# A hybrid attention, Mamba and expert layer on one core: the compressed branch moved into the compression stage, u loaded back in the attention stage, one more weight slot, and another order of the last expert pieces

## Chip, core and metric

The kernel runs on 1 core of one Trainium2 chip. The metric is device time in microseconds (us): the median of several executions. Engines are named as the profile names them: PE (TensorE), DVE (VectorE), ACT (ScalarE), POOL (GpSimd), SP (SyncE, which here issues most DMAs).

## What is computed

One layer over a prompt of 256 tokens and 8 samples of 8 tokens (320 rows of 1024). Cut to what matters here:

```python
xn = rmsnorm(x); q, kv, ag, z, xbc, dt, mg = split(xn @ w_in)
kc, vc = compress(cmp rows)                      # a row per 16 tokens, from blocks of 32
o_c = softmax(q @ kc.T - slope * dist) @ vc      # compressed branch
A = gate_c * o_c + gate_s * o_sel + gate_w * o_win
u = silu(causal_conv(xbc)); M = gated_norm(ssd_scan(u, dt), z)
h = x + (sigmoid(g_a) * (A @ Wa) + sigmoid(g_m) * (M @ Wm)) @ W_out
y = h + sum over the 2 experts (of 32) of each row: (silu(hn @ Wg) * (hn @ Wu)) @ Wd * weight
```

All is float32; where it says hi and lo below, a float32 matrix is split into two parts for three fast products in place of a slow one.

## The kernel before

The stages follow each other: x and the first projections (0 to 95 us); the compression of the caches of 8 samples and of the prompt (`st_cmp`, to 228); attention of the prompt (`st_prompt`, to 310); attention of the samples (`st_att`, to 421); the SSD (`st_ssd`); the merge and the output projection; the router; the experts (`ph_moe`, from 648 to the end).

Beside the middle stages runs a second stream, the fill (`st_fill`): the rest of the combined projection as 24 matmuls per tile of 128 columns, `mm<-xh,whl` and `mm<-xl,whl`. A tile needs its weights loaded (`w`, 1 MB for two tiles, two buffers, issued on SP) and split: hi by ACT (L342), lo by DVE (L343), into `whl`. `_drive` (L135) draws from the streams by costs written at each `yield`, and the framework's scheduler then fixes one order of instructions per engine. Each engine runs its own order strictly in a row, so an instruction that waits holds up all behind it on that engine. The same goes for a DMA that waits on the queue of SP.

The compressed branch of the prompt stands at the start of `st_prompt` (L929 ff.): PE multiplies KC and qT into tile `at`; DVE adds the distances (tile `PP` of `Pc`, L944), reduces (L945), clips, subtracts (L947) and scales (L951); ACT takes exp; DVE sums, inverts, applies the gate and normalises (L953 to L959, statistics in tile `cst`); PE transposes the result and ACT copies it to `PcT`, which every block of the prompt's attention then reads (`pv<-PcT,vcp`). The distances come by a DMA of 512 KB in `ph_b_setup` (L638). `q2_parts` (L650) splits q: ACT copies hi, POOL subtracts. Then follow 16 blocks of scores (`at<-K,q`), a fused add and maximum on DVE (L782 with tile `pmx`), exps on ACT, normalising, transposes (`tp<-PP`) and products (`pv`).

`ph_b2_setup` (L785) loads for the samples' attention the constants `cB` (932 KB) and `P`, after which `wraw` (512 KB) and the eight parts of `raw` follow, all on SP.

The fill writes u, the convolution's result, to DRAM (`ud`) and, per four feature tiles, the last raw rows (`cv`, L1110 ff.) to the outputs. `ph_c_setup` (L1146) loads half of u back (2 DMAs of 640 KB on ACT's queue) as the SSD starts; the SSD transposes it (`tp<-cA,u`).

The experts' weights come through a ring of 1 MB pieces: per expert four pieces of gate and up, (e,0) to (e,3), and two of down, (e,4) and (e,5). `RING_SLOTS` (L32) counts 18 slots. Pieces are loaded in the order of `rseq` (L1415 ff.), a piece when its slot is free; the first 18 while the stages ahead still run. Experts go in pairs; `gu` multiplies a piece when it is there, `turn` transposes, `down` multiplies the down pieces, `parts` splits the result, `scatters` adds it to the rows. In the last pair, `last_down` works with halves of columns. `back` (L1767) computes the scatter matrix and coefficients of a pair with small float32 products of `cr`.

## Time and profile before

| what | us |
|---|---|
| median of 3 runs | 1119.47 (1118.45 to 1124.41) |
| the profiled execution | 1119.53 |
| its span | 1117.8 |
| PE busy in it | 1057.1 |
| DVE busy in it | 618.2 |
| ACT busy in it | 409.6 |
| experts, from 648 us on | 470 |

The profiled execution lasted 1.7 us more than the span that the profile covers, and lies 0.06 us from the median. PE is busy in 95% of the span. An idle gap in a timeline stands in brackets behind the work that follows it, with what was waited for.

### The profile page before, as it was taken

How to read it: one execution, taken by the hardware profiler on the slowest of the kernel's cores; microseconds unless marked ns; L12 is line 12 of the kernel's file. 1: busy time of each engine (PE TensorE's matmuls, PEld its weight loads, DVE VectorE, ACT ScalarE, POOL GpSimd, SP SyncE). 2: the span in 40 equal slices, each digit the busy share in tenths (PEclk: the TensorE clock that was granted, in tenths of full speed). 3: DMA queues.
4: the chain of work that ended last, by engine and by line, in shares of the span. 5: the costliest groups of instructions: out<-in, count | busy, mean ns of one | idle time of the engine just before them, and what ended most of it. 6: DMA issues, size and time to landing. Idle time of an engine off the chain costs nothing.

```text
span 1117.8 us, 18377 instructions
## 1 busy us (share of the span) xinstructions
PE 1057.1 (95%) x6743; PEld 728.9 (65%) x6743; DVE 618.2 (55%) x1686; ACT 409.6 (37%) x959; POOL 85.0 (8%) x115
## 2 busy tenths in 40 slices
PE   6998999969999998999999989999999999999997
PEld 6898899957776787777899944354444444435333
DVE  4467777788867774578876532333434333333324
ACT  4446565677745452545545511110101010101101
POOL 3102000042200001024100000000000000000000
PEclk8999999989999998999999999999999999999999
DMA  7844555511266656584579969999999999999995
GB/s 213 229 139 141 164 153 155 149 56 55 87 181 204 196 153 191 155 229 91 138 267 342 375 211 411 413 414 413 411 412 414 413 414 413 412 412 414 413 413 197
DMA packets 141742, 298.01 MB, mean 267 GB/s; under 512 B 14918, under 2 KB 93222, under 8 KB 133970
## 3 DMA queue, kind: packets, MB, share of 16 engines
q1 hardware_dynamic: 135146, 283.34, 70.7%
q0 software_dynamic: 2688, 7.91, 2.3%
q10 hardware_dynamic: 3816, 5.56, 1.6%
q8 instruction: 55, 0.90, 0.3%
q14 instruction: 37, 0.30, 0.1%
HBM read 279.63 MB, written 15.29 MB: 264 GB/s over the span
## 4 chain that ended last, share of the span: by engine, by line


## 5 line engine op out<-in xcount | busy, mean ns | idle before, releaser
L215 PE MATMUL mm<-xh,whl 128*128 128x320 f32 (+1 forms) x1008 | 248.8, 326 | 7.6 <-ACT whl L342 4.4
L215 PEld LDWEIGHTS mm<-xh,whl 128*128 128x128 f32 (+1 forms) x1008 | 173.5, 191 | 21.1 <-issue 7.9
L215 PE MATMUL mm<-wr,xeT 128*64 128x512 f32 x752 | 171.8, 595 | 4.8 <-DMA wr<-in_w_exp_up 3.0
L215 PE MATMUL mm<-xl,whl 128*128 128x320 f32 (+1 forms) x504 | 162.9, 323 | 0.0
L215 PEld LDWEIGHTS mm<-wr,xeT 128*64 128x64 f32 x752 | 53.5, 137 | 109.8 <-issue 103.6
L215 PE MATMUL po<-wr,ehT 128*64 128x512 f32 (+1 forms) x448 | 118.5, 580 | 4.2 <-DMA wr<-in_w_exp_down 4.2
L343 DVE TENSOR_TENSOR whl<-w,whl 128x1024 fp32r<-128x1024 f32 (+1 forms) x79 | 96.0, 1217 | 23.7 <-ACT whl L342 22.5
L1805 DVE SCALAR_TENSOR_TENSOR eth<-eth,mm 128x256 f32<-128x256 f32 x31 | 13.1, 421 | 170.6 <-ACT eth L1804 170.6
L342 ACT ACTIVATE whl<-w 128x1024 fp32r<-128x1024 f32 (+1 forms) x79 | 83.1, 1055 | 45.8 <-PE mm L215 38.5
L215 PEld LDWEIGHTS mm<-xl,whl 128*128 128x128 f32 (+1 forms) x504 | 96.3, 191 | 3.3 <-issue 1.6
L1804 ACT ACTIVATE eth<-mm,cb 128x256 f32<-128x256 f32 x31 | 14.7, 475 | 201.0 <-PE mm L215 201.0
L215 PEld LDWEIGHTS po<-wr,ehT 128*64 128x64 f32 x448 | 37.3, 137 | 72.3 <-issue 60.3
L1858 DVE TENSOR_TENSOR ht<-sc,ht 128x512 f32<-128x512 f32 (+3 forms) x99 | 61.7, 665 | 38.7 <-PE sc L215 38.2
L215 PE MATMUL mm<-ah,whl 128*128 128x320 f32 x256 | 63.9, 322 | 0.0
L346 DVE SCALAR_TENSOR_TENSOR olo<-po,cb,ohi 128x512 fp32r<-128x512 f32 (+1 forms) x33 | 24.2, 734 | 49.7 <-ACT ohi L345 49.7
L1780 ACT ACTIVATE ohT<-tp 128x320 fp32r<-128x320 f32 x16 | 7.0, 437 | 106.1 <-PE sc L215 98.3
L215 PEld LDWEIGHTS mm<-ah,whl 128*128 128x128 f32 x256 | 43.9, 188 | 2.0 <-issue 0.7
L215 PE MATMUL tp<-oh,hh 128*128 128x256 f32 x192 | 42.2, 292 | 0.0
L215 PE MATMUL sc<-ohi,ohT 128*128 128x512 f32 (+3 forms) x99 | 41.5, 421 | 0.2
L345 ACT ACTIVATE ohi<-po,cb 128x512 fp32r<-128x512 f32 (+1 forms) x33 | 22.2, 674 | 53.1 <-PE po L215 53.1
L215 PE MATMUL mm<-al,whl 128*128 128x320 f32 x128 | 39.6, 309 | 0.0
L215 PEld LDWEIGHTS tp<-oh,hh 128*128 128x128 f32 x192 | 32.9, 188 | 9.0 <-issue 8.1
(491 smaller groups left out, 1895.0 us busy)
## 6 DMA issues: line engine op xcount, KB each, us to landing
wr<-in_w_exp_down SPq DMA_DIRECT2D x50, 1024.0 KB
wr<-in_w_exp_gate SPq DMA_DIRECT2D x98, 512.0 KB
wr<-in_w_exp_up SPq DMA_DIRECT2D x98, 512.0 KB
w<-in_w_in SPq DMA_DIRECT2D x23, 1024.0 KB
raw<-in_cache_kv SPq DMA_DIRECT2D x112, 128.0 KB
w<-in_w_exp_down SPq DMA_DIRECT2D x10, 1024.0 KB
whl<-in_w_exp_gate SPq DMA_DIRECT2D x20, 512.0 KB
whl<-in_w_exp_up SPq DMA_DIRECT2D x20, 512.0 KB
```

Source lines behind the costliest of these rows:

```text
L215: return s.nc.tensor.matmul(out, lhsT, rhs, start=start, stop=stop, skip_group_check=True)
L342: s.last_split = [nc.scalar.activation(hi, src, AF.Copy), nc.vector.tensor_tensor(lo, src, hi.bitcast(F32), op=OP.subtract)]
L343: nc.vector.tensor_tensor(lo, src, hi.bitcast(F32), op=OP.subtract)]
L345: nc.scalar.activation(hi, src, AF.Copy, scale=scale)
L346: nc.vector.scalar_tensor_tensor(lo, src, scale, hi.bitcast(F32), op0=OP.mult, op1=OP.subtract)
L1780: nc.scalar.activation(t, p[:, 0:T], AF.Copy)
L1804: nc.scalar.activation(hv, g, AF.Tanh, scale=hrs)
L1805: nc.vector.scalar_tensor_tensor(hv, hv, 1.0, g, op0=OP.add, op1=OP.mult)
L1858: nc.vector.tensor_tensor(y, ps[:m], y, op=OP.add)
```

## The change

- `st_pc` is a stream of its own that runs beside `st_cmp` as soon as the prompt's compressed keys are there (flag "kc"); it holds the whole compressed branch up to `PcT`. Its tiles Pc, PcT and cst lie in a new tile `ux`, and the DMA of the distances is issued ahead of the compression. `st_prompt` starts with the splits of K and of the first two parts of q; later parts of q are issued after an exp.
- u is loaded into the same memory (`ux`) by `load_x`, issued on SP: from the fill's z tiles as soon as the flag "prompt" is set, so within the samples' attention.
- To make room in memory some tiles share a buffer or have fewer (`gt`, `PT`, `qt`, `si`); `cv` is written per two feature tiles, in eight pairs of small DMAs in place of four.
- `RING_SLOTS` counts 19. The pieces (28,5) and (29,5) are loaded ahead of the four gate and up pieces of expert 31, and the products with them (`rest`) stand ahead of its `gu`; half of the scatters of that pair stand inside it.
- In `back` the three products with `cr` take hi and lo parts (`crs`, split once in the router's second part), with six columns in place of three, and the copies behind them become sums of three columns.

```diff
-RING_SLOTS = (8, 5, 2, 2, 1)
+RING_SLOTS = (8, 5, 2, 2, 2)
...
-        s.Pc = s.tl(P, [128, 1024], F32, "PP", bufs=3)
-        o, n = s.bo["pC"]
-        nc.sync.dma_start(s.Pc, s.I["cB"][:, o:o + n])
...
+    def ph_pc_setup(s):
+        t = s.tl(s.pU, [128, 8 * T], F32, "ux")
+        s.Pc = t[:, 0:1024]
+        s.PcT = t[:, 1024:2048].rearrange("p (a b) -> p a b", b=128)
+        s.cst = t[:, 2048:2144].rearrange("p (a b) -> p a b", b=32)
+        nc.sync.dma_start(s.Pc, s.I["cB"][:, o:o + n])
+
+    def st_pc(s):
+        yield lambda: "kc" in s.flags
...
+        for qt in range(2):
+            p = s.ps("tp", [128, 512])
...
+                s.mm(p[:, r * 64:r * 64 + n], s.qT[:, r, qt * 128:(qt + 1) * 128], KC[:, 0:n], True, True)
+            nc.vector.tensor_tensor(Pc[:, qt * 512:(qt + 1) * 512], p, Pc[:, qt * 512:(qt + 1) * 512], op=OP.add)
+            yield 3000
+        nc.vector.tensor_reduce(stt[:, 0], Pv, axis=AX.X, op=OP.max)
...
+        nc.scalar.activation(Pc, Pc, AF.Exp)
...
+        for hh in range(2):
+            p = s.ps("tp", [128, 4, 128])
+            for u in range(4):
+                s.tr(p[:, u], Pc[:, (hh * 4 + u) * 128:(hh * 4 + u + 1) * 128])
+            nc.scalar.copy(s.PcT[:, hh * 4:hh * 4 + 4], p)
+            yield 3000
...
-                if r % 2 == 0 and qt == 1 and r < 6:
-                    s.q2_parts(r + 2, r + 4)
                 cur = probs(r, qt)
+                if r % 2 == 0 and qt == 1 and r < 6:
+                    s.q2_parts(r + 2, r + 4, s.last_exp)
...
                 nc.sync.dma_start(s.zd[m // 2][m % 2], z)
+                if "prompt" in s.flags:
+                    s.load_x()
...
+    def load_x(s):
+        if not hasattr(s, "u"):
+            s.u = s.tl(s.pU, [128, 8 * T], F32, "ux").rearrange("p (f t) -> p f t", t=T)
+            for k in range(2):
+                s.nc.sync.dma_start(s.u[:, 4 * k:4 * k + 4], s.ud[k].rearrange("f p t -> p f t"))
...
-        s.u = s.tl(P, [128, 8, T], F32, "u")
-        for k in range(2):
-            nc.scalar.dma_start(s.u[:, 4 * k:4 * k + 4], s.ud[k].rearrange("f p t -> p f t"))
...
+        s.rseq[-6:] = s.rseq[-2:] + s.rseq[-6:-2]
...
-                mm(p[:, 384:387], o[i], s.cr[:, i, e // 2], i == 0, i == 2)
+                mm(p[:, 384:390], o[i], s.crs[:, i, e // 2].rearrange("p a b -> p (a b)"), i == 0, i == 2)
...
+            if e == 30:
+                left = rest()
+                after[1] = lambda: scatters(left[0], left[1])
             hB = gu(e + 1, lambda: cb[:, 2:3], after, "mm" if prev else "po")
-            if prev:
-                down(pe, st["hT"], 1, po)
-                left = (pt, *(parts(pe, po[dh], pcb[:, 0:1], dh * 512, 512) for dh in range(2)))
+            if prev and e < 30:
+                left = rest()
...
-    _drive([s.st_cmp()], [fill], RATES[0])
+    _drive([s.st_cmp(), s.st_pc()], [fill], RATES[0])
```

What this does to the order on three engines:

DVE at the start of the prompt's attention, before. `cst` and the rows of `PP_2336` are the compressed branch; `PP_2502`, `pmx_2503` and `PP_2522` are the first blocks of scores, on which PE's next matmuls wait for room.

```order
338 L945 TENSOR_REDUCE cst_2351<-PP_2336 128x32
339 L782 ISA PP_2502,pmx_2503<-at_2504,Dp_2334 128x128
340 L782 ISA pmx_2503 128x1
341 L946 TENSOR_SCALAR cst_2351<-cst_2351 128x32
342 L782 ISA PP_2502,pmx_2503<-at_2504,Dp_2334 128x128
343 L782 ISA pmx_2503 128x1
344 L947 TENSOR_TENSOR PP_2336<-PP_2336,cst_2351 128x1024
345 L782 ISA PP_2502,pmx_2503<-at_2504,Dp_2334 128x128
346 L782 ISA pmx_2503 128x1
347 L951 TENSOR_TENSOR PP_2336<-PP_2336,cA_11_110 128x512 x2
348 L994 TENSOR_TENSOR pmx_2503<-pmx_2503,cA_11_110 128x4
349 L782 ISA PP_2522,pmx_2523<-at_2524,Dp_2334 128x256
```

DVE after the change, in the compression: `ux_984` holds Pc and cst, `whl`, `cvt` and `ut` belong to the fill, `gt`, `gx`, `kx` to the compression.

```order
189 L671 TENSOR_TENSOR ux_984<-tp_1475,ux_984 128x512
190 L1114 SCALAR_TENSOR_TENSOR ut_2609<-raw_2607,cvt_2451 128x256
191 L673 TENSOR_REDUCE ux_984<-ux_984 128x32
192 L1115 SCALAR_TENSOR_TENSOR ut_2609<-raw_2607,cvt_2451 128x64
193 L674 TENSOR_SCALAR ux_984<-ux_984 128x32
194 L1090 MEMSET raw_2680 128x3
195 L676 TENSOR_TENSOR ux_984<-ux_984 128x1024
196 L714 SCALAR_TENSOR_TENSOR gt_1560<-gt_1560,gx_1558 128x256
197 L681 TENSOR_TENSOR ux_984<-ux_984,cA_11_110 128x512
198 L716 SCALAR_TENSOR_TENSOR gx_1558<-gt_1560,gx_1558 128x256
199 L681 TENSOR_TENSOR ux_984<-ux_984,cA_11_110 128x512
200 L790 COPY kx_203<-tp_1565 128x2x64
```

DVE after the change, at the start of the prompt's attention (`PP_2474`, `PP_2517`: the second and the third block of scores; the split of `whl` that PE's fill needs next follows as row 370).

```order
348 L1013 TENSOR_TENSOR pmx_2407<-pmx_2407,cA_11_110 128x4
349 L834 ISA PP_2474,pmx_2475<-at_2476,Dp_2387 128x256
350 L834 ISA pmx_2475 128x1
351 L834 ISA PP_2474,pmx_2475<-at_2479,Dp_2387 128x256
352 L834 ISA pmx_2475 128x1
353 L834 ISA PP_2474,pmx_2475<-at_2479,Dp_2387 128x256
354 L834 ISA pmx_2475 128x1
355 L834 ISA PP_2517,pmx_2518<-at_2519,Dp_2387 128x128
356 L834 ISA pmx_2518 128x1
357 L1013 TENSOR_TENSOR pmx_2475<-pmx_2475,cA_11_110 128x4
```

The compressed branch has left the rows between the first blocks of scores and stands among the compression's and the fill's rows.

SP before, at the border to the samples' attention.

```order
225 L1125 DMA zd_6_96<-ut_4208 128x320
226 L790 DMA cB_3705<-in_cB 128x1864
227 L794 DMA P_3708<-in_cB 32x1024
228 L799 DMA wraw_3711<-in_cache_win_kv 128x1024
229 L799 DMA wraw_3713<-in_cache_win_kv 128x1024
```

SP there after the change; `ux_4030` is u, in the memory from which PE reads PcT until the prompt's last block.

```order
232 L1134 DMA out_conv_prompt<-cv_3669 3x256
233 L1135 DMA out_conv_sample<-cv_3669 24x256
234 L1172 DMA ux_4030<-ud_1_91 128x4x320
235 L842 DMA cB_3678<-in_cB 128x1864
236 L846 DMA P_3681<-in_cB 32x1024
237 L851 DMA wraw_3684<-in_cache_win_kv 128x1024
238 L851 DMA wraw_3686<-in_cache_win_kv 128x1024
```

The first load of u stands ahead of `cB`, `P` and `wraw` (the second follows as row 258, behind the first `wraw` and `raw`).

PE before, at the end: the four pieces of expert 31 (`mm_10477`), then the second down pieces of pair 28 (`po_10467`, wr_1735 and wr_1736).

```order
3154 L215 MATMUL mm_10477<-wr_1717_10257,xeT_10176 64x512 x4
3155 L215 MATMUL mm_10477<-wr_1718_10264,xeT_10190 64x512 x4
3156 L215 MATMUL mm_10477<-wr_1730_10318,xeT_10204 64x512 x4
3157 L215 MATMUL mm_10477<-wr_1731_10325,xeT_10218 64x512 x4
3158 L215 MATMUL po_10467<-wr_1735_10342,ehT_10441 64x512
3159 L215 MATMUL po_10467<-wr_1736_10344,ehT_10441 64x512
```

PE there after the change: the down pieces come first (`po_10489`), and six scatters (`sc`) stand between the second and the third piece of expert 31 (`mm_10514`).

```order
3160 L215 MATMUL po_10489<-wr_1719_10265,ehT_10462 64x512
3161 L215 MATMUL po_10489<-wr_1725_10280,ehT_10462 64x512
3162 L215 MATMUL mm_10514<-w_10286,xeT_10199 64x512 x4
3163 L215 MATMUL mm_10514<-w_10340,xeT_10213 64x512 x4
3164 L215 MATMUL sc_10523<-ohi_10506,ohT_10308 128x512
3165 L215 MATMUL sc_10523<-olo_10507,ohT_10308 128x512
3166 L215 MATMUL sc_10527<-ohi_10506,ohT_10308 128x512
3167 L215 MATMUL sc_10527<-olo_10507,ohT_10308 128x512
3168 L215 MATMUL sc_10531<-ohi_10506,ohT_10308 64x512
3169 L215 MATMUL sc_10531<-olo_10507,ohT_10308 64x512
3170 L215 MATMUL mm_10514<-whl_10347,xeT_10227 64x512 x4
3171 L215 MATMUL mm_10514<-whl_10364,xeT_10241 64x512 x4
```

Behind the last piece of expert 31 there are left six scatters, the transposes and the last down.

## Rows read from the trace of the kernel before

**Rows 1.** the page, part 1: engine, busy us (share of the span), instructions.

```profile
PE 1057.1 (95%) x6743; PEld 728.9 (65%) x6743; DVE 618.2 (55%) x1686; ACT 409.6 (37%) x959; POOL 85.0 (8%) x115
```

**Rows 2.** windows by stage: stretch, us, busy of each engine, granted clock, DMA share, GB/s.

```profile
95.00:228.00 133.00, 127.67 (x955) 120.83 (x955) 99.50 (x238) 81.02 (x208) 7.90 (x25) 0.97 0.50 151
228.00:310.00 82.00, 70.66 (x555) 53.86 (x556) 71.75 (x282) 59.72 (x191) 26.55 (x24) 0.92 0.16 51
```

**Rows 3.** timeline of PE after 231 us: start, duration, work, [idle before <-releaser].

```profile
235.12 0.51 PE L215 MATMUL at<-K,q 128*128 128x256 f32 x2 [0.73 <-POOL q L656]
...
238.34 0.42 PE L215 MATMUL mm<-xh,whl 128*128 128x320 f32 x1 [1.50 <-ACT whl L342]
...
240.55 0.76 PE L215 MATMUL at<-K,q 128*128 128x512 f32 x2 [1.65 <-DVE pmx L782]
245.52 2.05 PE L215 MATMUL at<-K,q 128*128 128x256 f32 x6 [4.21 <-DVE pmx L782]
250.60 0.90 PE L215 MATMUL mm<-xh,whl 128*128 128x320 f32 x2 [3.03 <-DVE whl L343]
```

**Rows 4.** windows of 5 us around both waits.

```profile
235.00:240.00 5.00, 2.29 (x11) 1.67 (x11) 4.33 (x9) 4.90 (x10) 4.70 (x5) 1.00 0.00 0
240.00:245.00 5.00, 0.76 (x2) 0.30 (x2) 5.00 (x9) 1.57 (x3) 4.52 (x3) 0.61 0.00 0
245.00:250.00 5.00, 2.05 (x6) 1.35 (x6) 5.00 (x21) 3.59 (x17) 0.41 (x1) 0.50 0.00 0
250.00:255.00 5.00, 4.18 (x19) 3.64 (x20) 5.00 (x13) 1.44 (x4) 2.17 (x2) 0.53 0.67 207
...
435.00:440.00 5.00, 2.93 (x12) 2.67 (x13) 0.69 (x1) 0.00 (x0) 0.00 (x0) 0.56 0.59 154
440.00:445.00 5.00, 5.00 (x32) 4.81 (x30) 3.89 (x7) 0.13 (x1) 0.00 (x0) 0.76 0.08 16
```

**Rows 5.** VectorE's work on tile cst, in a window.

```profile
225.00:256.00 31.00, 7.66 (x9) 0.78 0.23 77
```

**Rows 6.** groups of instructions, VectorE, 228 to 256 us: busy, mean ns, idle before.

```profile
L951 DVE TENSOR_TENSOR PP<-PP,cA 128x512 f32<-128x512 f32 x2 | 3.2, 1645 | 0.0
...
L959 DVE TENSOR_TENSOR PP<-PP,cst 128x1024 f32<-128x1024 f32 x1 | 1.6, 1628 | 0.0
...
L944 DVE TENSOR_TENSOR PP<-at,PP 128x512 f32<-128x512 f32 x2 | 1.3, 686 | 0.0
```

**Rows 7.** groups of instructions, ScalarE, 226 to 256 us.

```profile
L655 ACT ACTIVATE q<-qT 64x512 fp32r<-64x512 f32 x8 | 5.0, 630 | 0.2
```

**Rows 8.** window within the compression.

```profile
135.00:195.00 60.00, 59.70 (x474) 56.87 (x473) 43.58 (x109) 33.53 (x92) 0.90 (x8) 1.00 0.48 145
```

**Rows 9.** timeline of PE where attention starts.

```profile
308.56 0.43 PE L215 MATMUL pv<-PcT,vcp 32*64 32x128 f32 x4
...
318.46 0.60 PE L227 MATMUL tp<-cA,wraw 128*128 128x128 f32 x4
```

**Rows 10.** window of 2 us there.

```profile
314.00:316.00 2.00, 2.00 (x16) 2.00 (x15) 1.09 (x9) 1.01 (x2) 1.00 (x1) 1.00 1.02 333
```

**Rows 11.** timeline of PE where the SSD starts.

```profile
437.07 1.08 PE L227 MATMUL tp<-cA,u 128*128 128x128 f32 x4 [4.51 <-DMA u<-ud]
```

**Rows 12.** windows at the experts' start and in their middle.

```profile
645.00:650.00 5.00, 4.38 (x28) 2.84 (x28) 4.04 (x21) 0.89 (x3) 0.00 (x0) 1.00 0.02 5
...
700.00:900.00 200.00, 200.00 (x1014) 89.66 (x1012) 74.49 (x170) 25.46 (x48) 0.00 (x0) 1.00 1.02 413
900.00:1100.00 200.00, 190.63 (x930) 84.61 (x926) 64.87 (x144) 24.57 (x46) 0.00 (x0) 1.00 1.02 410
```

**Rows 13.** timeline of PE at the end.

```profile
1092.71 3.65 PE L215 MATMUL po<-wr,ehT 128*64 128x512 f32 x14 [1.43 <-DMA wr<-in_w_exp_down]
1096.29 0.50 PE L215 MATMUL sc<-ohi,ohT 128*128 128x512 f32 x1
...
1100.26 5.38 PE L215 MATMUL po<-wr,ehT 128*64 128x512 f32 x32
```

More of the change, by code (lines that the diff above doesn't have):

```diff
@@ L654, in q2_parts @@
             hi = s.q2[R[g], g, a:b]
-            s.nc.scalar.activation(hi, q, AF.Copy)
+            with s.tc.issue_after(after.ins) if after is not None else nullcontext():
+                s.nc.scalar.activation(hi, q, AF.Copy)
             s.nc.gpsimd.tensor_tensor(s.q2[R[1 - g], g, a:b], q, hi.bitcast(F32), op=OP.subtract)
@@ L1720, in ph_r2 @@
         nc.vector.memset(s.cr[64:, 2], 0.0)
+        s.crs = s.tl(P, [128, 3, 16, 2, 3], F32R, "crs")
+        s.split(s.crs[:, :, :, 0], s.crs[:, :, :, 1], s.cr)
     def ph_moe(s, oh1, oh2, v8, last):
@@ L1905, in ph_moe, with rest @@
                 after[3] = nxt
+            def rest():
+                down(pe, st["hT"], 1, po)
+                return pt, *(parts(pe, po[dh], pcb[:, 0:1], dh * 512, 512) for dh in range(2))
+            if e == 30:
+                left = rest()
+                after[1] = lambda: scatters(left[0], left[1])
             hB = gu(e + 1, lambda: cb[:, 2:3], after, "mm" if prev else "po")
-            if prev:
-                down(pe, st["hT"], 1, po)
-                left = (pt, *(parts(pe, po[dh], pcb[:, 0:1], dh * 512, 512) for dh in range(2)))
+            if prev and e < 30:
+                left = rest()
             prev = e, (hA, hB), t, cb
         pe, hs, pt, pcb = prev
-        scatters(left[0], left[1])
+        scatters(left[0], left[2])
         phT = turn(hs)
-        scatters(left[0], left[2])
         s0 = last_down(pe, phT, pcb[:, 0:1], 0, 0, 512)
```

111 lines of the change are left out of this document (56 added, 55 removed).

## The prediction

> **What bounds the kernel now.** I read the page's busy times first, then windows by stage, then PE's timeline for its idle gaps, and last the windows that show the granted clock. PE is busy in 1057.1 of 1117.8 us [rows 1]: up to the experts PE's work and its gaps set the pace, and from then on the weights. The gaps sit in few places. The compression has PE busy 127.7 of 133 us, the prompt's attention only 70.7 of 82 [rows 2]. There the reader should see five gaps of 0.73, 1.50, 1.65, 4.21 and 3.03 us, 11.1 together, the last three for DVE [rows 3], and behind them the clock: 0.61, 0.50 and 0.53 of full speed, that is for the most part the 1.2 GHz level, from 240 to 255 us [rows 4]. The next long gap is 4.51 us at the start of the SSD, where PE waits for u out of DRAM [rows 11]; the clock falls to 0.56 and 0.76 there [rows 4]. From 700 us to 1100 the DMA share is 1.02 at 410 to 413 GB/s, PE never waits in the first 200 us and 9.4 us in the second [rows 12]: PE lives on a stock of pieces, and the DMA's last byte decides. Ahead of that, from 645 to 650, the DMA is idle at 5 GB/s, with all slots full [rows 12].
>
> **The change part by part**, against the profiled execution of 1119.53 us, practically the median.
>
> *A, the compressed branch.* Before: gaps 11.1 us, and time lost to the low clock, which is busy time times one less the granted share: 0.76 x 0.39 + 2.05 x 0.50 + 4.18 x 0.47 = 3.3 us [rows 4]. Together 14.4. The branch costs DVE 7.7 us on cst [rows 5] plus 3.2 and 1.3 [rows 6], 12.2 in all. Of these the two first adds (1.3) stand ahead of the first scores and the last product (1.6) behind the fill's split; so 9.3 us of DVE leave the 15.5 between the first gap's end at 235.1 and the split that ends the last gap at 250.6 [rows 3]. DVE is 100% busy in most of it [rows 4], but does not become empty: by the order the third block's four maxima move ahead of the split, for which I estimate 1.5 us (its share of what is left of the 15.5), so the split comes some 7.8 us earlier. The gaps behind the first score are 10.4 us [rows 3]; less 7.8, and with some 1.4 us of PE work that stood between them and now stands behind the split, 4 us stay. Ahead of the first score ACT copies two parts of q in place of eight (5.0 us for eight [rows 7]), yet the score stands 19 fill matmuls earlier in PE's order than before (744 ahead of it in place of 763), so I leave a gap of 2 us for K and q. Idle 6 in place of 11.1, and for such gaps 2 us at the low clock in place of 3.3: 8 stay of 14.4, a gain of 6.4. From 4 staying (gain 10) to 11 (gain 3) is open.
>
> The clock deserves a second look. The rows have DVE as what PE waited for, and the clock fell all the same [rows 3, 4]. The Trainium skill (TensorE: Matmul & The Clock Gate, section "Loop structure matters more than you think") sketches a DVE copy between matmul groups as harmless to the clock and a long DMA wait as what breaks it. By that, what returns at the prompt's start would be idle time alone, 5.1 us, and the sum 1.3 us smaller; this trace does not agree, and the sum goes by the rows.
>
> In the compression the 12.2 us meet a DVE busy for 43.6 of the 60 us from 135 to 195 [rows 8], which is about where the branch now runs: counted in fill matmuls along PE's order, its KC products stand where PE of before is at some 138 us, its transposes at some 197. 55.8 of 60 fit, but each engine works strictly in order and PE is full (59.7), so a part shows. Nearest price: the compression as a whole lost 5.3 us of 133 [rows 2]. Bounds 0 and 6 us (half the chain); I take 1.5, as the steps are spread between other rows and PE's own work (KC products, eight transposes) only moves. The early DMA of the distances, 512 KB ahead of the compression, falls into the loads of the start; I cost it at nothing. A = 6.4 - 1.5 = +5, from -1 to +9.
>
> *C, u loaded early.* It goes from ACT's queue at the SSD's start to SP in the samples' attention. The 4.51 us wait goes [rows 11], with the clock: 2.93 x 0.44 + 5.00 x 0.24 = 2.5 us [rows 4]. 7.0 in all. What is late next is DVE, which reads the same transposes; for that I take 0.5 off: +6.5, from 2.5 (a next wait of half the size, with the clock) to 7.
>
> *D, the queue that u is put on.* The first load of u stands on SP ahead of cB, P and wraw and waits for PE's last read of PcT, 308.56 us in the trace [rows 9]. Behind it 0.66 + 0.95 + 0.13 + 0.52 MB have to land before PE's transposes of wraw; at 333 GB/s, the rate of these loads [rows 10], 6.8 us, and some 2 us from issue to the first bytes. PE's order has fill up to there, 9.9 us from 308.56 to 318.46 [rows 9]: it just covers. DVE, which needs cB ahead of that, loses its lead. -1, from 0 to -4 (the cover short by 2, with the clock). The eight additional small output DMAs on SP, and the eight small copies on ACT for four larger ones, lie in stretches where neither is late: 0.
>
> *E, the 19th slot.* One piece is 1.049 MB, at 413 GB/s 2.54 us [rows 12]. It is loaded in the idle stretch at 645 to 650 us, waiting for no engine there, and all that follows on the saturated DMA ends that much earlier: +2.5, from 0 to 2.54. The Trainium skill (DMA: Bandwidth & Descriptors, section "Where 436 GB/s comes from") puts loads from HBM at about 358 GB/s; an estimate by that is 2.9 us for the piece and a sum 0.4 larger. The trace shows 413 and decides.
>
> *F, the last expert.* The wait that ends at 1092.71 is for the piece (29,5) [rows 13]; four pieces follow at 2.54 each, so (31,4) lands at 1097.8. Before, PE then has 16 down matmuls, twelve scatter matmuls, the transposes, and starts the last down at 1100.26 [rows 13]. Now (31,3) lands at 1092.7 in the place of (29,5), and there remain four matmuls, the activation chain, half of the scatters and the transposes, which I put at 1096.5: the last down starts when (31,4) is there, 1097.8. +2.5, from 0 to 3.9 (PE's old work from 1092.71 down to 1096.4).
>
> *G, `back`.* Fewer passes on PE, a split of crs in the router, sums for copies on DVE. In the experts PE has 9.4 us of waiting to give [rows 12]; around the router the split is small: 0, from -1 to +0.5.
>
> Sum: 5 + 6.5 - 1 + 2.5 + 2.5 = 15.5 us. The gains ahead of the experts carry on, since the prefetch of pieces is issued by the program's progress and all pieces of the old stock are in before 645 us [rows 12]. 1119.5 - 15.5 = **1104 us**.
>
> **Rivals.** (1) *The wait only moves.* DVE fills up in the compression and PE pays 6 there; A about 0.5: 1119.5 - 11 = 1108.5. For it: 55.8 of 60 us on one in-order engine [rows 5, 6, 8]. Against: the chain was at the very front of the work that PE waited for, now it has 60 us.
> (2) *The SP queue.* u's first load is late, cB and wraw behind it, PE runs out of fill: D at -6 (3.5 idle, 2.5 clock): 1109. For it: cover and need agree within 1.2 us. Against: PE's order has more fill in front of wraw than before.
> (3) *E and F don't show,* since the ring frees slots later or the last down waits for DVE: 1109. Against: the DMA share of 1.02 up to 1100 [rows 12].
> (4) *The prompt's start becomes nearly dense,* 3 us left of 14.4: 1099.
> (5) *Slower: the compression loses its clock.* If the moved DVE work stretches beyond the 4.2 us that are free in 135 to 195 [rows 5, 6, 8], PE gets a short wait at every step, the pattern of 235 to 250 us [rows 3], and works at the 1.2 GHz level as from 245 to 255 [rows 4]. Each us of work then takes two. With the other terms at +16.9 (6.4 + 6.5 - 1 + 2.5 + 2.5) it turns slower than 1125.1 from 22.5 us of loss, that is, some 20 of the 59.7 us of PE work at half speed with the waits; at 25 of work and 3 of waits the time is 1119.5 - 16.9 + 28 = 1130.6. Against: in the whole compression the clock is 0.97 [rows 2] with DVE at 75%.
>
> **How the numbers follow.** Forecast 0.50 (1101 to 1107); rival 1 0.13, rival 2 0.10, rival 3 0.07, rival 4 0.08; two of the losses together 0.08 (1114 to 1120); slower 0.04. Half a per cent, 5.6 us, is about what a measurement of this kernel can tell from no change: faster means under 1113.9. Faster 0.87, same 0.09, slower 0.04. The range leaves out about two in ten: 1097 to 1113.
>
> **What would show it.** A: the span from the first scores to the first products of the prompt shows gaps of 6 us or less in place of 11, DVE without the branch there; in the compression PE's gaps grow by under 3 us. C: no wait for u, the clock at 1.00 there. D: cB and wraw land late, PE waits under 2 us where attention starts. E: no idle DMA from 645 to 650, the DMA's end 2.5 us earlier relative to the experts' start. F: the last down starts when its piece lands. Wrong would make me: a gap at wraw of over 3 us, a clock below 0.9 through the compression, or a new wait ahead of the SSD.

## The result

The changed kernel takes 1110.9 us (median of 5, 1107.7 to 1112.3) against 1119.5; the ratio is 0.9899, with a 95% interval of 0.9876 to 0.9922. By the medians that is 8.6 us, by the ratio 11.3 (8.7 to 13.9). The forecast was 1104, a gain of 15.5. The time lies in the range of 1097 to 1113 and the side is right. The sum is not: the branch's move, one of its two largest terms, came out with the other sign, and a gain that the sum doesn't have took its place.

All experiments below are compared with the kernel before, measured beside them, by their ratio; 0.0010 of it is 1.1 us. Their intervals reach 0.0015 to 0.0023 to either side, so a difference between two of them is known to some 3 us. The profiled execution of after took 1108.69 us. Its page, part 1, beside [rows 1]: PE has 3.7 us less to do and the span is 11.0 us shorter.

```profile
PE 1053.4 (95%) x6695; PEld 722.2 (65%) x6695; DVE 616.4 (56%) x1687; ACT 419.6 (38%) x971; POOL 76.3 (7%) x115
```

The table cuts the profiled executions of both kernels and of five experiments, told of below, at the same landmarks in PE's timeline: the compression from 95 us to its last hh matmul (0.5 us behind that one's start); the prompt to its last pv; attention with the SSD's start to the last transpose of u; the rest of the SSD to the last transpose of ysq; the merge to the first transpose of hT; the router to the first expert matmul; the experts to the last scatter. The length stands first and, in brackets, what is lost in it: PE's idle time plus busy time times one less the granted clock, summed over short windows. Lengths also move where the scheduler deals the fill's matmuls out differently; losses move less with that, but each column is one execution, and between kernels whose code is the same in a stage its loss differs by up to 3.5 us (attention with the SSD's start: 1.1 in after, 4.6 in a_AC).

| us | before | after | b_si | a_noA | a_lateU | a_whl | a_best |
|---|---|---|---|---|---|---|---|
| compression | 125.7 (8.6) | 122.5 (3.1) | 119.3 (2.9) | 121.1 (4.0) | 121.7 (3.1) | 124.1 (3.1) | 124.0 (3.1) |
| prompt | 89.1 (14.6) | 87.3 (14.6) | 88.6 (14.2) | 88.9 (13.5) | 85.6 (13.0) | 84.5 (12.5) | 82.0 (8.4) |
| attention, SSD's start | 134.1 (9.3) | 120.6 (1.1) | 133.5 (7.9) | 128.6 (3.6) | 133.6 (8.8) | 120.8 (1.1) | 119.7 (1.0) |
| rest of the SSD | 117.1 (4.5) | 124.2 (5.0) | 117.2 (4.5) | 117.5 (3.0) | 125.7 (11.2) | 124.1 (4.8) | 123.3 (3.8) |
| merge | 41.5 (0) | 47.9 (8.0) | 41.5 (0) | 41.8 (0) | 48.6 (8.6) | 44.1 (4.0) | 44.1 (4.1) |
| router | 45.8 (3.1) | 45.5 (2.9) | 45.5 (2.8) | 45.5 (2.9) | 45.5 (2.9) | 45.5 (2.9) | 46.5 (4.1) |
| experts | 463.1 | 457.6 | 463.4 | 460.6 | 457.7 | 460.5 | 460.8 |

Read down the first two columns by what is lost: 5.5 us come back in the compression, none at the prompt, 8.2 up to the SSD's start, and the merge, where nothing was lost before, loses 8.0. The experts are 5.5 shorter. The prompt's 14.6 is the high end: five other kernels with the same code there (a_noC, a_ht, a_htw, a_whl, a_noE) lose 12.5 in their profiled executions, 6.9 idle and 5.6 to the clock, where after has 8.6 and 6.0, and before 11.4 and 3.2. So idle time went and the clock's loss grew in all of them, and some 2 us at most are left as a gain.

**The prompt's start.** PE's timeline of after, which answers [rows 3]: the waits are shorter, as forecast, and are now for POOL and DVE in turn.

```profile
230.34 0.97 PE L215 MATMUL at<-K,q 128*128 128x256 f32 x4 [1.73 <-POOL q L707]
...
233.81 4.43 PE L215 MATMUL at<-K,q 128*128 128x512 f32 x10 [0.79 <-DVE pmx L834]
239.35 0.56 PE L215 MATMUL mm<-xh,whl 128*128 128x320 f32 x2 [1.10 <-DVE whl L343]
244.26 1.29 PE L227 MATMUL tp<-cA,PP 128*128 128x128 f32 x8 [1.99 <-DVE PP L1029]
```

Windows of 5 us of after (PE busy first, the granted clock ahead of the last two figures), which answer the first four of [rows 4]. PE is busier in every one than before, and the clock is no better: 0.64 and 0.67, then 1.00 for a window, then 0.51 and 0.81 with PE busy 5.00 of 5.00. The low clock costs 1.3 + 1.3 + 2.5 + 0.9 = 5.9 us in place of 3.3.

```profile
230.00:235.00 5.00, 3.48 (x11) 2.44 (x12) 1.79 (x13) 3.82 (x14) 1.56 (x2) 0.64 0.00 2
235.00:240.00 5.00, 3.79 (x12) 1.96 (x10) 4.88 (x23) 4.47 (x18) 1.59 (x2) 0.67 0.00 0
240.00:245.00 5.00, 3.01 (x25) 2.46 (x26) 5.00 (x15) 2.48 (x11) 3.79 (x3) 1.00 0.00 0
245.00:250.00 5.00, 5.00 (x30) 3.68 (x29) 3.30 (x16) 3.49 (x9) 0.66 (x1) 0.51 0.00 0
250.00:255.00 5.00, 5.00 (x33) 3.32 (x32) 3.10 (x17) 2.77 (x13) 0.70 (x1) 0.81 0.02 6
```

**The merge.** PE's timeline of after shows two waits that the kernel before does not have, one for ACT's conversion of a weight, one for x coming back from memory:

```profile
565.43 0.41 PE L215 MATMUL mm<-xh,whl 128*128 128x320 f32 x1 [2.56 <-ACT whl L342]
568.63 1.09 PE L227 MATMUL tp<-cA,ht 128*128 128x128 f32 x4 [2.64 <-DMA ht<-in_x_prompt]
```

**The experts.** PE's timeline at the end of after, beside [rows 13]: the last down no longer stands behind old work, it waits 0.79 us for DVE's split of its input.

```profile
1088.31 0.44 PE L227 MATMUL tp<-cA,eth 128*128 128x128 f32 x2 [0.96 <-DVE eth L1836]
1089.53 5.38 PE L215 MATMUL po<-wr,ehT 128*64 128x512 f32 x32 [0.79 <-DVE ehT L1848]
```

### The profile page after: what moved, and what is told of

Same layout as the page of the kernel before. It is cut to its first block, busy times and chain, and to the rows that moved or that the text cites. A ratio compares the mean times of both kernels' runs of the same rounds, so it can differ in the third digit from the quotient of the medians.

```text
span 1106.8 us, 18296 instructions
## 1 busy us (share of the span) xinstructions
PE 1053.4 (95%) x6695; PEld 722.2 (65%) x6695; DVE 616.4 (56%) x1687; ACT 419.6 (38%) x971; POOL 76.3 (7%) x115
## 4 chain that ended last, share of the span: by engine, by line
## 5 line engine op out<-in xcount | busy, mean ns | idle before, releaser
L215 PE MATMUL po<-wr,ehT 128*64 128x512 f32 (+1 forms) x448 | 109.7, 588 | 5.7 <-DMA wr<-in_w_exp_down 4.9
```

Of the source, the lines that this page charges most:

```text
L215: return s.nc.tensor.matmul(out, lhsT, rhs, start=start, stop=stop, skip_group_check=True)
```

## The experiments

### The compression's start: one buffer moved (b_si)

The kernel before with one of the change's smaller edits alone, the one that lets the tile `si` share a buffer:

```diff
-si.append(s.tl(s.pst, [24, 1024], F32, "si", bufs=2))
+si.append(s.tl(s.pst, [128, 1024], F32, "xscr", bufs=3)[:24])
```

> The kernel before with one edit: the tiles si (the loaded conv state, 2 x 24 rows) lie in the buffers of xscr, as in the changed kernel. By the order of POOL this moves the tile pc to other memory, so that its first write waits for the DMAs that store kvtok (about 58 us in the trace after) and not for ACT's split of w1h (94.65 us in the trace before). Theory (the gain of 5.5 us at the compression's start in the trace after is a side effect of where pc lies): ACT's wait of 2.67 us for pc at 99.67 goes, PE's 2.40 us gap at 103.56 shrinks to about 0.6 and the clock stays at 1.00 in 100 to 130; about 1114 us, 5 below before. Rival (the gain there comes from the compressed branch's move or the queue's order): no change, 1119.5 us.

Measured: 1114.3 us, ratio 0.9955 (0.9938 to 0.9971). This one line is worth 5.0 us, though `si` is a small tile of the kernel's start. What it changes in the trace is another tile, `pc`, whose first write no longer waits for w1h; that pc got other memory by the shift is the reading, since nothing else differs between the two kernels. POOL's timeline of the kernel before: the clearing of pc waits until ACT's conversions of w1h are done at 94.65.

```profile
94.65 0.93 POOL L677 MEMSET pc<- 128x704 f32 x1 [41.52 <-ACT w1h L342]
```

ACT's timeline there: its next step waits for the copies that follow on POOL, and the conversions of w1h stand behind it in ACT's order.

```profile
99.67 0.35 ACT L342 ACTIVATE ch<-pc 128x176 fp32r<-128x176 f32 x1 [2.67 <-POOL pc L684]
99.92 1.05 ACT L342 ACTIVATE w1h<-ah 128x1024 fp32r<-128x1024 f32 x1
```

PE's timeline, and with it the clock (0.71 from 105 to 110 us):

```profile
103.56 0.86 PE L215 MATMUL hh<-ch,w1h 128*128 128x292 f32 x2 [2.40 <-ACT ch L342]
```

```profile
105.00:110.00 5.00, 5.00 (x29) 5.00 (x29) 4.96 (x12) 4.09 (x11) 0.00 (x0) 0.71 0.01 2
```

In the kernel of this run, POOL's timeline has the clearing 37 us earlier; PE's wait in that place is 0.59 us and the clock stays at 1.00. The trace of after shows the same, the clearing at 58.01 and a wait of 0.59 at 101.22.

```profile
57.09 0.68 POOL L677 MEMSET pc<- 128x704 f32 x1 [4.51 <-DMA out_win_sample<-kvtok]
```

```profile
100.10 0.86 PE L215 MATMUL hh<-ch,w1h 128*128 128x292 f32 x2 [0.59 <-ACT ch L342]
```

So 5 of the 11 us (3.2 to 6.9) come from a side effect of "making room", to which the prediction gives no term at all.

### The branch put back (a_noA)

The changed kernel, with the compressed branch at the prompt's start again and all else as changed:

```diff
+        s.flags.add("kc")
+        for _ in s.st_pc():
+            pass
...
+        yield 4500
...
-    _drive([s.st_cmp(), s.st_pc()], [fill], RATES[0])
+    _drive([s.st_cmp()], [fill], RATES[0])
```

> The changed kernel with the compressed branch emitted at the start of the prompt's attention again (same memory). PE's transposes of ht then stand behind 1704 fill matmuls as before, in place of 1562. Theory 1 (the move of the branch gained nothing at the prompt's start, 14.4 us lost in the trace before against 14.5 after, and costs at the merge by the early transposes): same time or up to 5 us less than the changed kernel, 1106 to 1112 us. Theory 2 (the prediction: the branch's move is worth 5 us): 1116 us. In both the prompt's start shows some 11 us of gaps again.

Measured: 1105.6 us, ratio 0.9868 (0.9851 to 0.9886). Without its main part the change is faster, by 3.5 us (0.2 to 6.7, if the two intervals are taken as independent). It is also 4.3 us (1.6 to 7.0) below a_noC, the next run, which has the branch moved and was measured beside it. The table says where: the merge loses nothing, and the prompt loses 13.5 us with the branch there against 12.5 to 14.6 in the nine kernels that have it moved and q split alike. The branch was not what the prompt's start hung on.

The 11 us of gaps that both theories expected did not come back: the prompt's idle time is 9.2 us in this run, against 11.4 in before. What else differs there is q. Before, POOL splits seven of q's eight parts beside the branch; in the changed kernel the later parts are held behind an exp, and in this run too. POOL's timeline of before:

```profile
233.80 10.86 POOL L656 TENSOR_TENSOR q<-qT,q 64x512 fp32r<-64x512 f32 x7
```

DVE's timeline of before, then of this run, for the same two scalings of the branch:

```profile
240.33 3.21 DVE L951 TENSOR_TENSOR PP<-PP,cA 128x512 f32<-128x512 f32 x2
```

```profile
234.42 1.29 DVE L681 TENSOR_TENSOR ux<-ux,cA 128x512 f32<-128x512 f32 x2
```

All of the branch's operations on DVE come to 8.7 us in this run, and to 8.7 in the compression of after; the 12.2 that the prediction took from [rows 5, 6] hold some 3.5 us by which they were longer with POOL at work beside them. The later parts of q are an edit of their own, which the sum doesn't price and no run takes alone.

### u loaded late (a_noC, a_lateU)

The first try put the load's code back to the SSD's start and on ACT's queue:

```diff
-                if "prompt" in s.flags:
-                    s.load_x()
...
-                s.nc.sync.dma_start(s.u[:, 4 * k:4 * k + 4], s.ud[k].rearrange("f p t -> p f t"))
+                s.nc.scalar.dma_start(s.u[:, 4 * k:4 * k + 4], s.ud[k].rearrange("f p t -> p f t"))
```

> The changed kernel with u loaded as the SSD starts, on ACT's queue, as before. Theory 1 (the gain at the SSD's start is given back in the merge, because the SSD ends earlier than the fill and its weight loads): PE waits about 4.5 us for u again, but the waits of 2.56 and 2.64 us at 565 and 568 us shrink; total at most 2 us above the changed kernel, 1111 to 1113 us. Theory 2 (the two are independent): 6 to 7 us above it, 1117 to 1118 us, with the merge's waits as they are.

Measured: 1109.7 us, ratio 0.9906 (0.9889 to 0.9922), as the changed kernel and below either theory. I took that for proof that the early load is worth nothing, and that was wrong: the scheduler issues the loads as soon as u's memory is free, wherever their code stands. The trace's issue rows of this run (count, then the first and last start) have them at 304.6 and 306.2 us, as early as in the changed kernel, where they start at 304.0 on SP:

```profile
L1170 ACTq DMA_DIRECT2D ux<-ud x2: 393/414/436, 304.6 to 306.2; - x2
```

So the run tells only that SP's queue or ACT's makes no difference beyond the intervals (step D). The late load has to be tied to something late:

```diff
+                s.att_split = s.last_split[0]
...
-                s.nc.sync.dma_start(s.u[:, 4 * k:4 * k + 4], s.ud[k].rearrange("f p t -> p f t"))
+                with s.tc.issue_after(s.att_split.ins):
+                    s.nc.scalar.dma_start(s.u[:, 4 * k:4 * k + 4], s.ud[k].rearrange("f p t -> p f t"))
```

> The changed kernel with u loaded late again: both loads are held on ACT's queue behind the last conversion of the samples' attention, as in the kernel before (the earlier run with this edit at the program's place alone issued them at 304.6 and 306.2 us all the same, so it left u early). Theory 1 (the prediction's term C: the early load takes off a wait of 4.5 us with 2.5 of clock behind it, whatever happens at the merge, whose waits hang on the return of x and on ACT's order): PE waits 4 us or more for u at the SSD's start, the merge stays at 47 to 48 us, 1115 to 1117.5. Theory 2 (what is gained at the SSD's start only makes the merge reach its loads earlier): the wait for u is back, the merge shrinks by as much, to 42 to 44 us, and the time is 1110 to 1112. Theory 3 (with the branch moved, PE's order has enough other work there to hide the load): no wait over 1 us for u, 1110 to 1112, merge 47 to 48.

Measured: 1119.8 us, ratio 0.9998 (0.9983 to 1.0014): the whole gain of the change is gone. The loads are issued at 411.5 and 411.9. PE's timeline has the wait back, in place of [rows 11]:

```profile
426.41 1.09 PE L227 MATMUL tp<-cA,ux 128*128 128x128 f32 x4 [3.69 <-DMA ux<-ud]
430.08 1.09 PE L227 MATMUL tp<-cA,ux 128*128 128x128 f32 x4 [0.99 <-DMA ux<-ud]
```

Its windows have the clock at 0.52 and 0.50 behind it:

```profile
425.00:430.00 5.00, 2.69 (x10) 2.31 (x10) 1.61 (x3) 0.00 (x0) 0.00 (x0) 0.52 0.77 262
430.00:435.00 5.00, 4.92 (x21) 4.43 (x22) 2.41 (x4) 0.00 (x0) 0.00 (x0) 0.50 0.40 82
```

Theory 1 has the mechanism, with a larger price than it gave: 11.1 us (8.0 to 14.2). The merge stays at 48.6, so nothing of u's gain is given back there. Theories 2 and 3 fall.

**Branch and load together.** With E, F and the moved buffer in all four, by ratio: branch moved and u early 0.9899 (after); u early alone 0.9868 (a_noA); branch alone 0.9998 (a_lateU); neither 0.9915, which was not run and is 0.9955 (b_si) less 0.0020 each for E and F (below). Measured by two kernels each are the early load with the branch moved, 11.1 us, and the moved branch's price with the early load, 3.5. The other two rest on the sum: the early load is worth 5.3 us with the branch in its old place, the moved branch costs 9.3 with the late load, each known to some 6 us. A second way, by a_AC below, gives 5.2 and 9.4 (for both moves together 1.7; 1.7 + 3.5, and 11.1 - 1.7). What the later parts of q and `back` (G) are worth is in the 5.3; no run takes them apart. In neither combination does the moved branch gain.

### The merge (a_ht, a_htw, a_whl)

With the branch moved and the order of the merge left alone (after, a_noC, a_noE, a_noF, a_AC, a_lateU) the merge takes 47.9 to 48.6 us; with the branch at the prompt (before, b_si, a_noA, a_noAq) 41.5 to 41.8. What differs is PE's order: the first transposes of ht, the x that is loaded back, stand behind 1370 of the fill's 1512 matmuls `mm<-xh,whl` and `mm<-xl,whl` with the branch moved, behind all of them without (the expectation counts 192 more ahead of both). POOL's timeline of before and of after has the load's issue, and PE's of before the transposes: 30 us from the one to the other before, 9.2 in after (559.44 to 568.63).

```profile
566.01 0.71 POOL L1551 DMA_DIRECT2D ht<-in_x_prompt  x1 [17.21 <-DVE ga L1486]
```

```profile
596.31 0.58 PE L227 MATMUL tp<-cA,ht 128*128 128x128 f32 x3
```

```profile
559.44 0.71 POOL L1579 DMA_DIRECT2D ht<-in_x_prompt  x1 [22.64 <-DVE xl L343]
```

Run a_ht holds the first two blocks' transposes behind the fill's last matmul:

```diff
-            for i, m in enumerate(NT):
-                s.tr(xT[:, i * 128:i * 128 + m], ht[:m, i, f * 128:(f + 1) * 128], m)
+            with s.tc.issue_after(s.lastmm.ins) if f < 2 else nullcontext():
+                for i, m in enumerate(NT):
+                    s.tr(xT[:, i * 128:i * 128 + m], ht[:m, i, f * 128:(f + 1) * 128], m)
```

> The changed kernel with the first two groups of transposes of ht put behind the fill's last matmul on PE, as they stood before. Theory 1: the wait of 2.64 us for the load of x at 568.6 us goes, and with it most of the 2.3 us lost to the low clock behind it: 1106 to 1108 us. Theory 2 (the weights of the merge are late anyway, and PE waits for the next one instead): within 1 us of the changed kernel, 1110 to 1112 us.

Measured: 1105.8 us, ratio 0.9884 (0.9865 to 0.9903). The wait for ht is gone and the merge is at 44.9 us in place of 47.9. Between the two ratios lie 1.7 us, less than their intervals tell apart; the stage shows 3.0. Theory 1 has the wait right; the ratios alone don't exclude theory 2.

The other wait, for ACT's conversion, stayed at 2.55. Run a_htw takes a competitor off the DMA:

```diff
-RING_AHEAD = (1, 2, 1, 1, 3, 5, 0)
+RING_AHEAD = (0, 3, 1, 1, 3, 5, 0)
```

> The changed kernel with the first two column blocks of ht held behind the last fill matmul of the fill's pass (which took the wait for ht off), and one ring piece that was loaded beside the merge's weights moved to the next point of the program. Theory 1 (three transfers, w_branch_ssm, the first ring piece and the return of x, share the DMA at 1.06 ahead of the merge, so without the piece the weights for w_branch_ssm land 2 to 2.5 us earlier and ACT's conversion with them): the gap of 2.6 us that ACT's conversion of that weight ends goes too, with its clock loss: the merge 41.5 to 43 us, 1103 to 1105. Theory 2 (ACT's own conversions ahead of it decide when that weight is ready): the gap stays at 2 us or more, and the time is that of the kernel with ht held alone, 1105.8.

Measured: 1106.2 us, ratio 0.9873 (0.9852 to 0.9893), the wait at 2.55: theory 2, the ring piece on the DMA is not it. ACT's timeline of after shows what is: both conversions stand behind two `ah` that wait for DVE's gm, and gm waits for PE.

```profile
560.88 0.47 ACT L345 ACTIVATE ah<-gm 128x320 fp32r<-128x320 f32 x1 [3.17 <-DVE gm L1552]
563.96 0.47 ACT L345 ACTIVATE ah<-gm 128x320 fp32r<-128x320 f32 x1 [2.61 <-DVE gm L1552]
564.34 1.99 ACT L342 ACTIVATE whl<-w 128x1024 fp32r<-128x1024 f32 x2
```

So a_whl, on top of a_ht, puts the first of these conversions ahead of the second `ah`:

```diff
-                s.split(s.ah[:, f], s.al[:, f], m, scale=0.5)
+                with s.tc.issue_after(s.last_split[0].ins) if f < 2 else nullcontext():
+                    s.split(s.ah[:, f], s.al[:, f], m, scale=0.5)
```

> The changed kernel with the first two column blocks of ht held behind the fill's last matmul, and the merged block's ah placed behind the next weight's conversion whl on ACT. Theory 1 (the gap of 2.55 us at the merge is ACT's order: whl stands behind two ah that wait for DVE, while its weight has long landed): the gap goes, with 1.4 us of clock behind it: the merge 41 to 42.5 us in place of 44.9, 1102 to 1103. Theory 2 (the weight w itself lands only at 560.5 and the order is no cause): the gap stays at 2 us or more, 1105.8.

Measured: 1104.9 us, ratio 0.9852 (0.9832 to 0.9873), and PE still waits 1.95, now for DVE. ACT's timeline has the conversion done at 561.2:

```profile
560.18 1.04 ACT L342 ACTIVATE whl<-w 128x1024 fp32r<-128x1024 f32 x1
```

DVE's has the low half of the same weight behind the two steps on gm, which wait for PE's current group to end:

```profile
561.84 0.49 DVE L1551 SCALAR_TENSOR_TENSOR gm<-gm,mm 128x320 f32<-128x320 f32 x1 [1.04 <-PE mm L215]
562.36 0.49 DVE L1552 TENSOR_TENSOR gm<-gm,ga 128x320 f32<-128x320 f32 x1
562.77 1.22 DVE L343 TENSOR_TENSOR whl<-w,whl 128x1024 fp32r<-128x1024 f32 x1
```

The same mistake of order on the next engine: neither theory had that. The merge is at 44.1, so of the 8.0 us that it lost, 4.0 are back. To hold DVE's step back too was not tried.

### The ring and the last expert (a_noE, a_noF)

```diff
-RING_SLOTS = (8, 5, 2, 2, 2)
+RING_SLOTS = (8, 5, 2, 2, 1)
```

> The changed kernel with the ring back at 18 slots. Theory 1 (the experts live on a stock of pieces and the last byte of the DMA decides): one piece, 2.5 us, moves back behind 650 us, and the time from the first expert's start to the end grows by 2.0 to 2.6 us; with the changed kernel at 1110.9 that is 1113.4. Theory 2 (the stretch from 645 to 650 us and the end are bound by PE's own order, the stock matters no more): the time from the experts' start to the end stays within 0.7 us of the changed kernel's, 1111. Both: nothing changes ahead of the experts beyond the spread between executions.

Measured: 1111.0 us, ratio 0.9919 (0.9899 to 0.9940): 2.2 us for the slot, within the intervals of either theory. Its profiled execution has the experts at 460.5 us, 2.9 longer than after, but no longer than in five of the kernels that have the slot (460.5 to 460.8). The idle DMA that [rows 12] show from 645 to 650 us stands at 640 to 645 in this kernel (5 GB/s), and the 19th piece is loaded there in after (80 GB/s). The window of a_noE, then that of after:

```profile
640.00:645.00 5.00, 4.38 (x28) 2.81 (x26) 4.24 (x22) 1.24 (x4) 0.00 (x0) 1.00 0.02 5
```

```profile
640.00:645.00 5.00, 4.38 (x27) 2.80 (x27) 4.23 (x22) 1.24 (x4) 0.00 (x0) 1.00 0.20 80
```

Run a_noF puts the last expert's order back:

```diff
-        s.rseq[-6:] = s.rseq[-2:] + s.rseq[-6:-2]
...
-            if e == 30:
-                left = rest()
-                after[1] = lambda: scatters(left[0], left[1])
...
-            if prev and e < 30:
+            if prev:
```

> The changed kernel with the last but one pair's last down again after the first half of the last expert, and the rest of the last expert in the old order. Theory 1 (the end was set by PE's old work behind the wait for that piece, which the new order takes off): the last down starts later against the DMA's last byte, and the experts' part grows by 2.5 us (1 to 3.9): 1113.4. Theory 2 (what ends last in the changed kernel is the chain of the activation on DVE and the transposes behind it, as long as the old work): within 0.7 us, 1111.

Measured: 1112.4 us, ratio 0.9919 (0.9904 to 0.9934), again 2.2 us. The intervals don't settle either of the two alone; by the medians of the same runs in place of the ratios neither gains anything. The experts take 462.1 us here. The traces do settle both together: the experts take 457.6 to 460.8 us in the nine kernels that have both (mean 459.6) and 462.8 to 463.4 in the three that have neither (mean 463.1): 3.5 us, where 5 were forecast.

### Only the branch and the early load (a_AC)

The changed kernel with E and F undone, and with POOL's clearing of pc tied to w1h again (the compression loses 6.9 us in this run, 8.6 in before):

```diff
-        nc.gpsimd.memset(pc, 0.0)
+        w = s.w1h[:, 0, 8:16, 0:88].bitcast(F32)
+        nc.gpsimd.tensor_tensor(pc.rearrange("p a b c -> p (a b c)").rearrange("p (x y) -> p x y", x=8), w, w, op=OP.subtract)
```

> Of the change only the branch beside the compression and u's early load stay (with the smaller edits around the merge): the ring has 18 slots, the last expert has its old order, and the clearing of the tile pc on POOL is tied to the same late wait that it had in the kernel before (it subtracts a piece of w1h from itself), so that the compression's start waits as before. Theory 1 (the branch's move returns nothing net at the prompt's start, and what u's load returns at the SSD's start is given back at the merge; the 8.6 us of the change are the compression's start and the last expert): 1119 to 1122, no difference from the kernel before beyond 0.3%. Theory 2 (the prediction's terms: +5, +6.5 and -1): 1109.

Measured: 1118.6 us, ratio 0.9985 (0.9966 to 1.0003), 1.7 us less than before. That is theory 1's time within its 0.3%, not the 1109 of the prediction's terms. It also checks the sum: 11.3 less 2.2, 2.2 and 5.0 leaves 1.9. But theory 1 gave the wrong reason. By a_lateU nothing of u's load is given back: the load gains some 5 and the branch takes 3.5.

### Why the prompt's start kept its loss (a_best, a_noAq)

Run a_best is a_whl with the low halves of q computed on DVE:

```diff
-            s.nc.gpsimd.tensor_tensor(s.q2[R[1 - g], g, a:b], q, hi.bitcast(F32), op=OP.subtract)
+            s.nc.vector.tensor_tensor(s.q2[R[1 - g], g, a:b], q, hi.bitcast(F32), op=OP.subtract)
```

> As the kernel with whl ahead of ah, and the low parts of q at the prompt's start computed on DVE (0.70 us for 64x512 there) in place of POOL (1.28). Theory 1 (PE's waits at the prompt's start of 1.73, 0.39 and 0.39 us are for POOL, and POOL at work stretches DVE's 128x4 operations from 0.16 to 1.24 us): the prompt's stage loses 2.5 us of idle less, and up to 4.5 us of clock more if the short gaps were what took it: 1097 to 1100. Theory 2 (DVE is what is full there, so 5.6 us more on it lengthen its chain by what POOL's waits give back): within 1 us of the kernel with whl ahead of ah.

Measured: 1103.9 us, ratio 0.9849 (0.9827 to 0.9872): the time is theory 2's, no different from a_whl, though the intervals leave room for 3.7 us of gain. The stage is nearer to theory 1: the prompt loses 8.4 us in place of 12.5, and all of the clock's share of it, 5.6, is back. Its windows, to set against those of after above:

```profile
230.00:235.00 5.00, 2.93 (x16) 2.18 (x16) 4.32 (x16) 4.93 (x13) 0.00 (x0) 1.00 0.01 3
235.00:240.00 5.00, 5.00 (x33) 4.47 (x31) 4.52 (x28) 4.92 (x19) 0.78 (x1) 1.00 0.00 0
240.00:245.00 5.00, 3.29 (x29) 2.31 (x27) 4.91 (x20) 4.12 (x13) 1.03 (x1) 1.00 0.00 0
```

PE is busy for less of these windows than in after and has its full clock; the scheduler now deals the fill's matmuls out between the scores. The stage is 2.5 us shorter than a_whl's; the profiled execution loses 3.1 us to the clock from 630 to 640 us, in the router and the first expert, where a_whl's loses none, and the times can't tell 2.5.

Run a_noAq makes the same edit on a_noA, with the branch at the prompt's start.

> The changed kernel with the compressed branch back at the prompt's start, and the low parts of q on DVE. Theory 1 (with the branch, DVE is the chain there, and POOL worked beside it): no gain, 1105.6 or up to 3 us longer. Theory 2 (POOL's waits and its slowing of DVE cost the same with the branch there): 2.5 to 5 us shorter than without that edit, 1101 to 1103.

Measured: 1107.5 us, ratio 0.9880 (0.9860 to 0.9900), against 0.9868 without the edit: theory 1, no gain. There PE waits for DVE's chain longer than in a_noA (2.60 and 1.33 us for pmx, where the longest for DVE was 1.00).

**The best version** is a_best or a_whl, which can't be told apart; their intervals lie below the changed kernel's. Nor can they be told from a_noA, which leaves the branch's move out in place of mending what it does to the merge.

## Why the prediction was right, and where its sum was wrong

The side and the range are right. That the range holds is luck in good part: without the 5.0 us of the moved buffer, which the prediction did not know of, the time would be near 1116 (an estimate from b_si), above its 1113. Of the sum, in the order early load, branch, ring, last expert, by ratio:

| step | forecast | measured |
|---|---|---|
| A, branch beside the compression | +5 | -3.5 |
| C, u early | +6.5 | +5.3, with q and G in it (11.1 if the branch is moved first) |
| D, SP's queue | -1 | 0 |
| E, 19th slot | +2.5 | +2.2, not clear of noise alone |
| F, last expert | +2.5 | +2.2, not clear of noise alone |
| G, `back` | 0 | no run |
| buffers shared | not priced | +5.0 |
| sum | 15.5 | 11.2 |

The measured column adds up to the change's 11.3 because its steps are differences along one chain of ratios; what checks it is a_AC.

*A* is the step that failed, and its -3.5 holds the merge's loss, told of below. At the prompt's start the idle time was right: 6 us were to stay, and 6.2 did from 225 to 260. The clock was not: "2 us at the low clock in place of 3.3" turned out 5.9. I had taken the clock's loss to go down with the waits, and it went up. The Trainium skill (TensorE: Matmul & The Clock Gate, section "Loop structure matters more than you think") sketches a DVE copy between groups of matmuls, with the next ones following immediately, as harmless to the clock. That is not the case of before, which the prediction holds against it, nor of after: there PE waits 0.39 to 1.73 us for POOL and DVE between groups, and the windows show 0.64 and 0.67. No run here shows the sketch's own case. In a_best waits of 0.2 to 1.3 us went with 1.00. Second, the small waits for q and PP from 261 to 281 us (0.38, 0.41, 0.68 and 0.68) were not counted: they come to 2.2 us, and with 6.2 and 5.9 make the 14.3 that are as much as the 14.4 before. Third, the 12.2 us that the branch takes from DVE are 8.7 without POOL's splits beside it, and 2.2 of the prompt's idle time are gone in a_noA too, where the branch stands in its old place: part of what the move was to give back came with the later parts of q, as far as one execution of each tells.

The price of 1.5 us in the compression was too high: it loses 3.1 us with the branch and 2.9 in b_si without it. The 55.8 of 60 us of DVE were not reached. The window of [rows 8] in after has 48.93, and the clock stayed at 1.00 where rival 5 had it fall:

```profile
135.00:195.00 60.00, 59.81 (x471) 57.41 (x470) 48.93 (x116) 33.94 (x92) 0.90 (x8) 1.00 0.47 137
```

*"The gains ahead of the experts carry on"* is the sentence that hid the loss. It was argued from the prefetch of pieces, and no gap was looked for between the SSD's end and the router. There the moved branch changes where the scheduler puts ht's transposes and the weight's conversions, and 8.0 us are lost. The order of the changed kernel showed ht's transposes 142 fill matmuls earlier, which was the sign to look there. The trace of before would still have priced the wait at about nothing: ht lands 6.6 us behind its issue there, and in after 9.05, with 2.64 of wait, while loads of w and of two ring pieces issued from 558.4 to 559.4 are under way beside it.

*C* was right in mechanism, and in size with the branch in its old place: the SSD's start lost 4.5 us of waiting and 2.6 of clock in before, from 425 us on, and loses nothing in after; by the times it is 5.3. That it is worth twice as much with the branch moved was not foreseen. *D*: no wait at wraw; rival 2 did not come. *E* and *F* together are right in kind, 3.5 to 4.4 us in place of 5. F's reason was half right: the last down waits for DVE, not for its piece. Rivals 1, 2 and 3 gave 1108.5 to 1109, nearest to the time. The mechanisms of 1 and 2 did not appear, and rival 3, that E and F don't show, is answered only for the two together, by the 3.5 us.

What stays open: why the scheduler places ht's transposes earlier with the branch moved; and why the moved branch costs 9.3 us without the early load. The table puts that in the rest of the SSD (11.2 lost in place of 4.5), where PE waits for a state's load, for DVE and for a weight's split in turn, and which comes first was not tested.

## What to carry to other kernels

Price the edits that "make room" as well: a tile that moves in memory takes over the waits of what lay there, and here that was worth 5 of 11 us. Moving a chain off the engine that PE waits for gives back only what no other engine is late for, and the clock has to be priced again with the waits that remain. Where a scheduler sets the order, read it to the end of the program and not at the edited place alone, and see in the trace that an experiment's undone part is undone: a load whose code was put back was still issued 107 us early.

## What the runs showed of the hardware

A POOL operation that runs beside it can make a DVE operation long. DVE's timeline of after: the same operation on 128x4 takes 0.17 us alone and 1.25 us where POOL has just begun on q; another takes 0.15 alone and 0.82 beside POOL.

```profile
236.82 0.17 DVE L828 TENSOR_SCALAR pmx<-pmx 128x4 f32<-128x4 f32 x1
...
238.01 0.15 DVE L1023 TENSOR_TENSOR pmx<-pmx,gtok 128x4 f32<-128x4 f32 x1
...
239.97 1.25 DVE L828 TENSOR_SCALAR pmx<-pmx 128x4 f32<-128x4 f32 x1
...
242.02 0.82 DVE L1023 TENSOR_TENSOR pmx<-pmx,gtok 128x4 f32<-128x4 f32 x1
```

POOL's timeline there:

```profile
239.85 2.97 POOL L707 TENSOR_TENSOR q<-qT,q 64x512 fp32r<-64x512 f32 x2
```

The Trainium skill (SBUF — State Buffer, section "SBUF: two separate sides") calls the ports that DVE and POOL share an exclusive lock: of a POOL operation and a DVE operation that needs these ports, the one that starts first holds them for its whole instruction. The trace agrees: the two long operations end at 241.22 and 242.84, and POOL's two at 241.19 and 242.82. The fused add and maximum that reads the scores from `at` (L834, 128x256) takes 0.41 to 0.42 us either way.

The clock was at half speed, its 1.2 GHz level, in windows that the record shows as full: 0.51 from 245 to 250 us in after, with PE busy 5.00 of 5.00, behind a wait of 1.99 us. At the SSD's start of a_noC it fell with no wait before it: PE was busy 19.96 of the 20 us from 395 to 415, and what it did from 415.28 to 419.99, apart from 0.71 us on 128 columns, were matmuls of 8 and 16 columns. The windows of a_noC, then those of after around the same matmuls (413.13 to 417.40), where the clock stayed:

```profile
415.00:420.00 5.00, 5.00 (x38) 4.75 (x37) 0.65 (x4) 0.53 (x4) 1.18 (x2) 0.90 0.94 286
420.00:425.00 5.00, 5.00 (x25) 4.79 (x24) 1.14 (x2) 1.40 (x3) 1.97 (x3) 0.50 1.08 319
```

```profile
410.00:415.00 5.00, 5.00 (x57) 4.82 (x54) 2.77 (x9) 1.69 (x8) 2.82 (x4) 1.00 1.00 319
415.00:420.00 5.00, 5.00 (x44) 4.85 (x44) 0.83 (x2) 1.57 (x4) 2.85 (x4) 1.00 1.02 292
```

The same loss of 3.4 us stands there in a_noA and a_AC, and it is most of the 3.6 in a_noA's column of the table. So the clock was not the same each time PE did the same work. From 38 to 95 us, too, where the changed kernel, a_noA, a_noC, a_ht and a_noAq are the same, their profiled executions lost between 0 and 5.0 us to it; the five times of the changed kernel spread over 4.6.
